# Encoder block on one core: neighbourhood attention in four shifted query groups of two key blocks each, and the later modulation as output columns summed on VectorE

## The chip, the cores and the metric

The kernel runs on one core of one Trainium2 chip. The metric is device microseconds of one execution. TensorE is PE in the profile, VectorE DVE, ScalarE ACT, GpSimd POOL, and SyncE, whose queue issues most transfers, SP.

## The reference, cut to what matters

512 tokens of width 2048 pass through one block: a modulation vector from the conditioning `c`, a normalized and modulated input, one projection for two attentions and two gates, the attentions, an output projection, a SwiGLU, and a last norm.

```
mod = c_act @ w_ada + b_ada                     # c_act = silu(c); 6 parts of 2048
sh1, sc1, g1, sh2, sc2, g2 = split(mod, 6)
h  = rms_norm(x, norm1_w) * (1 + sc1) + sh1
qa, ka, va, qb, kb, vb, ga, gb = split(h @ w_in)
ya = global_gqa(...)                            # 8 heads, all 512 keys
yb = neighbourhood_attention(qb, kb, vb, rpb)   # 8 heads: each query sees 8 rows x 16 columns
merged = sigmoid(ga) * (ya @ w_oa) + sigmoid(gb) * (yb @ w_ob)
x  = x + g1 * (merged @ w_out)
h2 = rms_norm(x, norm2_w) * (1 + sc2) + sh2
x  = x + g2 * ((silu(h2 @ w_ffn_gate) * (h2 @ w_ffn_up)) @ w_ffn_down)
return rms_norm(x, final_w)
```

The tokens form a grid of 8 rows and 64 columns. In the neighbourhood attention a query sees all 8 rows and the 16 columns that begin 8 to its left, moved inwards at the grid's edges, with a learned bias by relative row and column.

## The kernel before, in words

Products are made in 32-bit form with a split: each operand is parted into a high part (a copy on ScalarE, line 133) and a rest (a subtraction on VectorE, line 134), and `mm3` makes three products (lines 141 to 143). Weights arrive as `raw` tiles of 128x1024 (512 KB) over SP's queue, are split into `whl`, and are multiplied. `form1` and `form2` are the loops over a weight matrix; behind each weight tile they call `pump`, which advances a background list `bg` by `pace["steps"]` steps and calls functions due from `soon` (a total is put there to run one pump later). A scheduler then sets the order on each engine and mixes independent work, so that the products of the gates and projections stand between those of the attentions. Tokens are in column order: 8 tokens to a grid column, so a block of 128 tokens is 16 columns.

Stages by time in the profile: the first modulation, the norm and the first projections (0 to 300 us), the global attention `att_a` (300 to 430), the gate products `sg_b` (430 to 560), the neighbourhood attention `att_b` with its own projections (560 to 820), more gates (820 to 920), the output projections of both attentions (`gated`, 920 to 1115), `w_out` (1115 to 1300), and the SwiGLU (to the end).

The neighbourhood attention, head by head (`att_b`, lines 635 to 659): four blocks of 128 queries, which see 2, 3, 3 and 2 blocks of keys (`KR`). For each block: three score products of 256 or 384 columns into a bank `S`, scale and bias on VectorE (line 646), a softmax (lines 557 to 568), a 128x128 transposition for each key block (line 650) into bank `T`, and a split into `pt`. Then, key block by key block, three products of 256 or 384 columns into `Y` (lines 656 to 658). The bias of a head is put together on the chip (`bias_of`): 16 transfers of 8 rows each on SP's queue into `braw` (line 625), and three additions of a mask on GpSimd (line 630).

The later modulation (`sh2`, `sc2`, `g1`, `g2`, each 2048 long) is background work of 128 steps. A step loads 1024 columns' worth of `w_ada` (line 285) and multiplies two pieces of 128x512 by a column of `c_act`, adding them into `acc` (line 300, and line 298 for a first piece). So the sum over partitions is still open, and TensorE closes it: `ada_mod.total` with four products of one column for each of 8 groups (line 319), `ada_gate.total` with one product of 512 columns in plain 32-bit form for each of 8 quarters (line 332). The gates are written to memory (line 335) and read back as rows.

The first modulation (line 401) is done in the other way already: rows of transposed weights, `ada1_w`, are multiplied by `call`, which holds `c_act` along the free axis in all partitions, and summed by the same VectorE instruction.

Of the kernel before, what the change touches and what calls it, by code (L numbers as in the profile page):

```python
# [13 lines left out]
F32 = mybir.dt.float32  # L14
F32R = mybir.dt.float32r
AF = mybir.ActivationFunctionType
# [3 lines left out]
P = 128  # L20
# [16 lines left out]
RPB_R, RPB_C = 2 * ROWS - 1, 2 * WIN - 1  # L37
TB_PAD = 240
TB_LEN = 945
TB_RUN = 720  # L40
# [16 lines left out]

def rope_tables():
# [13 lines left out]
def window_masks():  # L72
    def block(i, b0, b1):
        m = np.full((P, (b1 - b0) * P), NEG, np.float32)
        for p in range(P):
            col = i * WIN + p // ROWS
            cs = min(max(col - HALF, 0), GRID_W - WIN)
            for kc in range((i + b0) * WIN, (i + b1) * WIN):
                if cs <= kc < cs + WIN:
                    o = (kc - (i + b0) * WIN) * ROWS  # L80
                    m[p, o:o + ROWS] = 0.0
        return m

    return np.concatenate([block(1, -1, 2), block(0, 0, 2), block(NT - 1, -1, 1)], axis=1)
# [3 lines left out]
def encoder_block(ctx: ExitStack, tc, xp, xT, c, w_ada, ada1_w, b_ada, norm1_w, w_in, q_norm_w, k_norm_w, tb,  # L88
                  w_oa, w_ob, w_out, norm2_w, w_gate, w_up, w_down, final_w, rope, wmask, out):
# [184 lines left out]
    accp = aside  # L274
    def ada_units(cols, w):

        nj = len(cols)
        nk = 1024 // (nj * w)

        for k0 in range(0, KT, nk):  # L280
            raw = raw_tile()
            r4 = raw.rearrange("p (k c n) -> p k c n", k=nk, c=nj)
            for j, col in enumerate(cols):
                src = w_ada[k0 * P:(k0 + nk) * P, col:col + w]
                nc.sync.dma_start(r4[:, :, j], src.rearrange("(k p) n -> p k n", p=P))
            yield [(k0 + e, raw[:, e * nj * w:(e + 1) * nj * w]) for e in range(nk)]

    def ada_acc(cols, w, bias):


        acc = accp.tile([P, 512], F32, tag="acc", name="acc", bufs=2)[:, :len(cols) * w]
        if bias:
            G.memset(acc, 0.0)
            nc.sync.dma_start(acc[0:1, :], b_ada[:, cols[0]:cols[0] + w])
        for parts in ada_units(cols, w):
            for k, part in parts:
                if k == 0 and not bias:
                    V.tensor_scalar(acc, part, cact[:, k:k + 1], None, op0=ALU.mult)
                else:
                    V.scalar_tensor_tensor(acc, part, cact[:, k:k + 1], acc, op0=ALU.mult, op1=ALU.add)  # L300
            yield None
        yield acc

    def ada_done(y, k0, n, s, b_s, nw, t, b_t):
        sl = slice(k0, k0 + n)
        V.tensor_add(s[:, sl], y[:, :n], b_s[:, sl])
        V.tensor_add(t[:, sl], y[:, n:2 * n], b_t[:, sl])
        V.scalar_tensor_tensor(s[:, sl], s[:, sl], 1.0, nw[:, sl], op0=ALU.add, op1=ALU.mult)

    def ada_mod(sh, sc, k0, n, to):  # L310

        for acc in ada_acc((sc + k0 * P, sh + k0 * P), n * P, False):
            if acc is None:
                yield

        def total():
            y = bank("Y")
            for j in range(2 * n):
                nc.tensor.matmul(y[:, j:j + 1], acc[:, j * P:(j + 1) * P], ones[:, 0:1], start=True, stop=True)
            ada_done(y, k0, n, *to)  # L320

        soon.append((1, total))

    def ada_gate(col, q, dst):

        for acc in ada_acc((col + q * 512,), 512, True):
            if acc is None:
                yield

        def total():  # L330
            y = bank("Y")
            nc.tensor.matmul(y, ones, acc, start=True, stop=True)
# [33 lines left out]
    call = p_x.tile([P, D], F32, name="call")  # L366
# [238 lines left out]
    bg.extend(ada_mod(3 * D, 4 * D, k, 2, (s2, b_sc2, n2, t2, b_sh2)) for k in range(0, KT, 2))  # L605
    g1_d, g2_d = ([dram.tile([1, 512], F32, name=f"g{n}d{q}") for q in range(4)] for n in (1, 2))
    bg.extend(ada_gate(2 * D, q, g1_d) for q in range(4))
    bg.extend(ada_gate(5 * D, q, g2_d) for q in range(4))
# [7 lines left out]
    msk = p_b.tile([P, 7 * P], F32, name="msk")  # L616
    nc.sync.dma_start(msk, wmask)
    KR = [(0, 2), (0, 3), (1, 4), (2, 4)]
    MS = [3 * P, 0, 0, 5 * P]

    def bias_of(h):
        raw = p_b.tile([P, 768], F32, tag="braw", name="braw", bufs=1)[:, :TB_RUN]
        for cc in range(WIN):
            o = (WIN - 1 - cc) * RPB_R
            nc.sync.dma_start(raw[cc * ROWS:(cc + 1) * ROWS, :], tb[h * ROWS:(h + 1) * ROWS, o:o + TB_RUN])
# [9 lines left out]
    def att_b(h, q, k, v, vs):  # L635
        bm = bias_of(h)
        pt = [t.rearrange("p (k q) -> p k q", k=NT) for t in pair(p_b, "pt", NT * T, 1)]
        for i in range(NT):
# [10 lines left out]
            for j in range(k1 - k0):  # L649
                nc.tensor.transpose(tp[:, j * P:(j + 1) * P], e[:, j * P:(j + 1) * P], ident)  # L650
# [628 lines left out]
```

## Time and profile before

| | |
|---|---|
| timed runs | 2579.44, 2584.04, 2613.58 us; median 2584.04 |
| span of the profiled execution, first to last instruction | 2582.4 us |
| time of that execution outside its span | not recorded |
| PE busy | 2539.9 us, 98% of the span, 16573 instructions |
| weight loads of PE | 2294.9 us, 89% |
| DVE busy | 1921.5 us, 74% |
| ACT busy | 1026.9 us, 40% |
| POOL busy | 94.6 us, 4% |
| bytes read and written | 412.03 MB and 44.06 MB |

PE's busy time is the union of records that overlap (each matmul's record is longer than its distance to the next), so the distance from one start to the next tells what a product costs. A plain 32-bit product stands as two records.

### The profile page before, as it was taken

The numbers are of one execution on the slowest core, as the hardware profiler recorded it, in microseconds if no ns is written. First come the engines' busy times: TensorE is split into PE (matmuls) and PEld (weight loads), VectorE is DVE, ScalarE is ACT, GpSimd is POOL, SyncE is SP. The second block draws the span as 40 slices with busy tenths as digits, with TensorE's granted clock in tenths as the row PEclk, the third lists the DMA queues.
The fourth block names the chain that finished last, engine by engine and source line by source line (L and its number), as shares of the span: only waits on it lengthen the run. The fifth ranks groups of instructions, "written<-read, shape, count | busy, mean of one in ns | idle before, by whom it ended". The sixth has DMA issues, their size and how long they took to land.

```text
span 2582.4 us, 40993 instructions
## 1 busy us (share of the span) xinstructions
PE 2539.9 (98%) x16573; PEld 2294.9 (89%) x16573; DVE 1921.5 (74%) x2712; ACT 1026.9 (40%) x1404; POOL 94.6 (4%) x134
## 2 busy tenths in 40 slices
PE   7999999999999999999999999999999999999998
PEld 5888878888887887878999999999999998999997
DVE  8985787766645665665798888888888885687867
ACT  5223544223333322225754444444444454334333
POOL 0100000001010000011000000000000000001000
PEclk8999999999999999999999999999999999999999
DMA  9864245975534866776444434443444456547472
GB/s 352 304 227 146 66 155 164 305 235 167 164 100 149 287 219 205 249 256 213 131 139 131 129 120 129 131 129 101 133 130 130 127 192 209 176 144 248 160 256 98
DMA packets 251950, 458.77 MB, mean 178 GB/s; under 512 B 16113, under 2 KB 102497, under 8 KB 243313
## 3 DMA queue, kind: packets, MB, share of 16 engines
q1 hardware_dynamic: 238208, 381.64, 46.2%
q0 software_dynamic: 12064, 71.31, 7.7%
q10 hardware_dynamic: 1488, 3.20, 0.4%
q8 instruction: 130, 2.13, 0.3%
q14 instruction: 60, 0.48, 0.1%
HBM read 412.03 MB, written 44.06 MB: 177 GB/s over the span
## 4 chain that ended last, share of the span: by engine, by line
PE 78%; DMA 7%; DVE 6%; issue 6%; ACT 1%; POOL 0%; SPq 0%; DVEq 0%; POOLq 0%; ACTq 0%
PE mm L141 16%; PE mm L143 16%; PE mm L142 16%; PE S L141 6%; PE S L143 6%; PE S L142 6%; DMA raw<-in_w_ada 4%; PE Y L141 2%; PE Y L142 2%; PE Y L143 2%; DVE whl L134 1%; DVE acc L300 1%; DMA raw<-in_w_down 1%; PE T L143 1%; PE T L141 1%
## 5 line engine op out<-in xcount | busy, mean ns | idle before, releaser
L133 ACT ACTIVATE whl<-raw 128x1024 fp32r<-128x1024 f32 (+1 forms) x483 | 463.9, 962 | 820.1 <-PE mm L143 266.8
L134 DVE TENSOR_TENSOR whl<-raw,whl 128x1024 fp32r<-128x1024 f32 (+1 forms) x483 | 532.0, 1111 | 227.7 <-ACT whl L133 219.2
L300 DVE SCALAR_TENSOR_TENSOR acc<-raw,cact,acc 128x512 f32<-128x512 f32 x248 | 188.2, 759 | 86.3 <-DMA raw<-in_w_ada 79.3
L134 DVE TENSOR_TENSOR whl<-ta,whl 128x1024 fp32r<-128x1024 f32 x104 | 127.3, 1224 | 71.2 <-ACT whl L133 70.0
L133 ACT ACTIVATE whl<-tb 128x1024 fp32r<-128x1024 f32 x104 | 110.7, 1065 | 157.8 <-PE S L143 131.2
L133 ACT ACTIVATE whl<-ta 128x1024 fp32r<-128x1024 f32 x104 | 110.5, 1062 | 150.5 <-PE mm L143 114.0
L134 DVE TENSOR_TENSOR whl<-tb,whl 128x1024 fp32r<-128x1024 f32 x104 | 127.0, 1221 | 11.3 <-ACT whl L133 8.7
L856 DVE TENSOR_TENSOR ta<-raw 128x512 f32<-128x512 f32 x104 | 71.7, 690 | 37.0 <-DMA raw<-in_w_down 34.8
L141 PE MATMUL mm<-whl,s 128*128 128x256 f32 x320 | 88.8, 279 | 4.6 <-DVE acc L1132 4.6
L141 PE MATMUL mm<-x3h,whl 128*128 128x256 f32 x336 | 92.7, 276 | 0.0
L142 PE MATMUL mm<-x3l,whl 128*128 128x256 f32 x336 | 92.7, 276 | 0.0
L143 PE MATMUL mm<-x3h,whl 128*128 128x256 f32 x336 | 92.7, 276 | 0.0
L141 PE MATMUL mm<-x56h,whl 128*128 128x256 f32 x336 | 92.7, 276 | 0.0
L142 PE MATMUL mm<-x56l,whl 128*128 128x256 f32 x336 | 92.7, 276 | 0.0
L143 PE MATMUL mm<-x56h,whl 128*128 128x256 f32 x336 | 92.7, 276 | 0.0
L141 PE MATMUL S<-x56h,whl 128*128 128x256 f32 x336 | 92.7, 276 | 0.0
L142 PE MATMUL S<-x56l,whl 128*128 128x256 f32 x336 | 92.7, 276 | 0.0
L143 PE MATMUL S<-x56h,whl 128*128 128x256 f32 x336 | 92.7, 276 | 0.0
L857 DVE TENSOR_TENSOR ta<-raw,ta 128x512 f32<-128x512 f32 x104 | 71.6, 688 | 27.2 <-DMA raw<-in_w_down 23.1
L142 PE MATMUL mm<-whl,s 128*128 128x256 f32 x320 | 88.9, 278 | 0.0
L143 PE MATMUL mm<-whl,s 128*128 128x256 f32 x320 | 88.7, 278 | 0.0
L858 DVE TENSOR_TENSOR tb<-raw 128x512 f32<-128x512 f32 x104 | 71.6, 688 | 3.4 <-DMA raw<-in_w_down 1.5
(1504 smaller groups left out, 8510.3 us busy)
## 6 DMA issues: line engine op xcount, KB each, us to landing
raw<-in_w_in SPq DMA_DIRECT2D x133, 512.0 KB
raw<-in_w_gate SPq DMA_DIRECT2D x92, 512.0 KB
raw<-in_w_up SPq DMA_DIRECT2D x88, 512.0 KB
raw<-in_w_down SPq DMA_DIRECT2D x88, 512.0 KB
raw<-in_w_ada SPq DMA_DIRECT2D x128, 256.0 KB
raw<-in_w_ada SPq DMA_DIRECT2D x64, 512.0 KB
raw<-in_ada_w POOLq DMA_DIRECT2D x29, 1024.0 KB, 6.5
raw<-in_w_out SPq DMA_DIRECT2D x48, 512.0 KB
```

The source lines that it names most:

```text
L133: S.activation(hi, src, AF.Copy)
L134: eng.tensor_sub(lo, src, hi)
L141: nc.tensor.matmul(o, lh, rh, start=start, stop=False, **kw)
L142: nc.tensor.matmul(o, lh, rl, start=False, stop=False, **kw)
L143: nc.tensor.matmul(o, ll, rh, start=False, stop=stop, **kw)
L300: V.scalar_tensor_tensor(acc, part, cact[:, k:k + 1], acc, op0=ALU.mult, op1=ALU.add)
L856: V.tensor_sub(t1, b12, b11)
L857: V.tensor_sub(t2_, b22, t1)
L858: V.tensor_sub(t3, b22, b12)
```

## The change

**Neighbourhood attention.** The query groups are shifted by 64 tokens: group 0 holds the last 64 and the first 64 tokens, groups 1, 2 and 3 the 128 tokens that straddle two neighbouring key blocks. Each group then sees two key blocks (group 0: blocks 0 and 3). All products of scores and values have 256 columns. Two groups share one bank, so the softmax of a head runs in two passes over 512 columns (with two exponentials of 256 each), in the order (1, 2), (0, 3). The bias with its mask comes ready from memory, one transfer of 128x512 a head on POOL's queue. The queries get 64 more columns, a copy of the last 64 tokens ahead (two ScalarE copies of 64 columns a head). In the value products, the one for key block 2 writes two separate runs of 128 columns of the bank.

**Later modulation.** All four parts are laid out as rows of output columns (`ada2_w`), multiplied by `call` and summed by one VectorE instruction for each 128x1024. Both kinds of total lose their products; the two gates get one transposition of 128x16 each, a transfer of the bias part, an addition, and four stores. `call` moves from a pool of the first stage to `aside`, and is copied once to `call2`.

```diff
+def later_columns(w):
+    return np.concatenate([ada_columns(w[:, 3 * D:5 * D]), w[:, 2 * D:3 * D].T, w[:, 5 * D:].T])
...
-    def ada_acc(cols, w, bias):
...
-                    V.scalar_tensor_tensor(acc, part, cact[:, k:k + 1], acc, op0=ALU.mult, op1=ALU.add)
...
-                nc.tensor.matmul(y[:, j:j + 1], acc[:, j * P:(j + 1) * P], ones[:, 0:1], start=True, stop=True)
...
+    def ada_columns_sum(b0, n):
+        for j in range(b0, b0 + n):
+            for e in range(2):
+                raw = raw_tile()
+                cs = slice(e * 1024, (e + 1) * 1024)
+                nc.sync.dma_start(raw, ada2_w[j * P:(j + 1) * P, cs])
+                V.scalar_tensor_tensor(raw, raw, 1.0, call[:, cs], op0=ALU.mult, op1=ALU.mult,
+                                       accum_out=mcol[:, 2 * j + e:2 * j + e + 1])
                 yield
...
         def total():
-            y = bank("Y")
-            nc.tensor.matmul(y, ones, acc, start=True, stop=True)
+            yp = bank("Y")
+            nc.tensor.transpose(yp[:KT, :P], y, ident)
             o = io.tile([P, 512], F32, tag="io", name="ada_o")
-            V.tensor_copy(o[0:1, :], y[0:1, :])
-            nc.sync.dma_start(dst[q], o[0:1, :])
+            nc.sync.dma_start(o[:KT, :P], row(b_ada[:, col:col + D]))
+            V.tensor_add(o[:KT, :P], o[:KT, :P], yp[:KT, :P])
+            for q in range(4):
+                nc.sync.dma_start(dst[q].rearrange("o (k p) -> (o k) p", p=P), o[4 * q:4 * q + 4, :P])
...
+    bg.extend((ada_mod(), ada_gate(2 * KT, 2 * D, g1_d), ada_gate(3 * KT, 5 * D, g2_d)))
...
     def att_b(h, q, k, v, vs):
-        bm = bias_of(h)
...
+        bm = p_b.tile([P, 512], F32, tag="bm", name="bm", bufs=2)
+        nc.gpsimd.dma_start(bm, bias[h * P:(h + 1) * P, :])
...
+        for gs, b2, o in (((1, 2), inner, 512), ((0, 3), edge, 0)):
             sc = bank("S")
+            for n, g in enumerate(gs):
+                mm3(by(sc)[:, 2 * n:2 * n + 2], *(rows_of(t, g) for t in q), *(keys_of(t, g) for t in k), True, True)
...
+            V.scalar_tensor_tensor(s2v, sc.rearrange("p (g n) -> p g n", g=2), SCALE, b2, op0=ALU.mult, op1=ALU.add)
+            V.reduce_max(mx, s2v, axis=AX.X)
...
+            for j, at in enumerate((0, 1, 2, 3) if o else (2, 3, 1, 0)):
+                nc.tensor.transpose(tp[:, j * P:(j + 1) * P], e[:, at * P:(at + 1) * P], ident)
+            split(*(t[:, o:o + 512] for t in pt), tp)
         yb = bank("Y")
+        for n, (kk, at, to) in enumerate(((1, slice(5, 7), slice(2, 4)), (0, slice(3, 5), slice(1, 3)),
+                                          (2, slice(0, 8, 7), slice(0, 4, 3)), (3, slice(1, 3), slice(0, 2)))):
+            mm3(by(yb)[:, to], v[kk][0][:, vs], v[kk][1][:, vs], *(by(t)[:, at] for t in pt), n == 0, n == NT - 1,
+                skip_group_check=True)
...
+    def queries(hi, lo, b):
+        split(hi[:, 64:], lo[:, 64:], b)
+        for t in (hi, lo):
+            S.activation(t[:, :64], t[:, T:], AF.Copy)
```

Three places show how the change moves instructions. In the new program the same lines of code stand about 2 lower near `split` and `mm3` (131 for 133, 139 to 141 for 141 to 143), 24 lower in the global attention (540 for 564), and 23 lower in `gated` (690 for 713).

The first place is PE in the output projection of the first attention (`y3h` and its like are the split outputs of its heads). Before, a total of a gate stands between two triples:

```order
L143 MATMUL mm<-y3h,whl 128x512
L332 MATMUL Y<-acc,ones 128x512
L141 MATMUL mm<-y4h,whl 128x512
L142 MATMUL mm<-y4l,whl 128x512
L143 MATMUL mm<-y4h,whl 128x512
```

Now there is one of these for all of `g1`, and it is a transposition (`ysum` holds the 16 sums of each partition):

```order
L140 MATMUL mm<-y7l,whl 128x512
L141 MATMUL mm<-y7h,whl 128x512
L306 MATMUL Y<-ident,ysum 16x128
L139 MATMUL mm<-y8h,whl 128x512
L140 MATMUL mm<-y8l,whl 128x512
```

Eight products of 512 columns became two transpositions, and the 32 products of one column (line 319) have no successor on PE.

The second place is DVE at the first two heads of the neighbourhood attention, from the last split of the keys on. Before (`sb` scores with bias, `mx` the maximum, `sm` and `rs` the sum and its reciprocal, `e` the exponentials):

```order
L646 SCALAR_TENSOR_TENSOR sb<-S,bm 128x256
L646 SCALAR_TENSOR_TENSOR sb<-S,bm 128x384
L560 TENSOR_REDUCE mx<-sb 128x1 x2
L561 TENSOR_SCALAR mx<-mx 128x1
L300 SCALAR_TENSOR_TENSOR acc<-raw,cact,acc 128x512
L561 TENSOR_SCALAR mx<-mx 128x1
L134 TENSOR_TENSOR whl<-raw,whl 128x1024
L300 SCALAR_TENSOR_TENSOR acc<-raw,cact,acc 128x512
L566 RECIPROCAL rs<-sm 128x1
L646 SCALAR_TENSOR_TENSOR sb<-S,bm 128x384
L567 TENSOR_SCALAR e<-e,rs 128x256
```

Now, each row over two groups:

```order
L607 SCALAR_TENSOR_TENSOR sb<-S,bm 128x512 x2
L609 TENSOR_REDUCE mx_4850<-sb 128x2
L609 TENSOR_REDUCE mx_4877<-sb 128x2
L610 TENSOR_SCALAR mx_4850<-mx_4850 128x2
L132 TENSOR_TENSOR whl<-raw,whl 128x1024
L610 TENSOR_SCALAR mx_4877<-mx_4877 128x2
L281 SCALAR_TENSOR_TENSOR raw,mcol<-raw,call 128x1024
L615 RECIPROCAL rs_4852<-sm_4851 128x2
L607 SCALAR_TENSOR_TENSOR sb<-S,bm 128x512
L617 TENSOR_SCALAR e<-e,rs_4852 128x256 x2
```

The bias, the maximum and the division of two groups stand together, with the split of a weight tile and one modulation step between them and the first `e` that can be transposed.

The third place is ACT in the global attention (`pth` the split of the transposed exponentials, `st` the split of the values, `g` a gate that `gated` loads and passes through a sigmoid). Before:

```order
L564 ACTIVATE e,sm<-S,mx 128x512
L133 ACTIVATE whl<-raw 128x1024
L133 ACTIVATE pth<-T 128x4x128
L564 ACTIVATE e,sm<-S,mx 128x512
L133 ACTIVATE whl<-raw 128x1024
L133 ACTIVATE pth<-T 128x4x128
```

Now:

```order
L540 ACTIVATE e,sm<-S,mx 128x512
L131 ACTIVATE whl<-raw 128x1024
L690 ACT_TABLE_LOAD
L690 ACTIVATE g<-g 128x512
L131 ACTIVATE pth<-T 128x4x128
L131 ACTIVATE st<-st 128x256
L540 ACT_TABLE_LOAD
L540 ACTIVATE e,sm<-S,mx 128x512
```

Two gates of the later stage `gated` moved up into the attention, and each sigmoid between exponentials brings two table loads. Two further sigmoids (`go`, the gates of `sg_a`) are parted by an exponential where they stood side by side. ACT has 19 table loads in all, where it had 13.

More of the change, by code (lines that the diff above doesn't have):

```diff
@@ L272, in encoder_block @@
     t2 = const.tile([P, KT], F32, name="t2")
[L274 to L286, printed above, removed]
@@ L288, in ada_acc @@
-    def ada_acc(cols, w, bias):
[L291 to L302, printed above, removed]
@@ L324, in ada_gate @@
[L324 to L332, printed above, removed]
+    mcol = const.tile([P, 8 * KT], F32, name="mcol")
+    def ada_columns_sum(b0, n):
[6 more added lines that the diff above has]
+                                       accum_out=mcol[:, 2 * j + e:2 * j + e + 1])
+                yield
@@ L703, in encoder_block @@
     gate = gpool.tile([P, D], F32, name="gate1")
-    accp = gpool
+    first_call, call = call, gpool.tile([P, D], F32, name="call2")
+    S.activation(call, first_call, AF.Copy)
     mx = [pair(p_m, f"m{j}", 1024, 1) for j in range(KT // 2)]
```

140 lines of the change are left out of this document (57 added, 83 removed).

## Prediction

> **What bounds the kernel now.** I read the page first: busy times, then the chain that ended last by engine and by line.
>
> ```profile
> span 2582.4 us, 40993 instructions
> ...
> PE 2539.9 (98%) x16573; PEld 2294.9 (89%) x16573; DVE 1921.5 (74%) x2712; ACT 1026.9 (40%) x1404; POOL 94.6 (4%) x134
> ...
> PE 78%; DMA 7%; DVE 6%; issue 6%; ACT 1%; POOL 0%; SPq 0%; DVEq 0%; POOLq 0%; ACTq 0%
> PE mm L141 16%; PE mm L143 16%; PE mm L142 16%; PE S L141 6%; PE S L143 6%; PE S L142 6%; DMA raw<-in_w_ada 4%; PE Y L141 2%; PE Y L142 2%; PE Y L143 2%; DVE whl L134 1%; DVE acc L300 1%; DMA raw<-in_w_down 1%; PE T L143 1%; PE T L141 1%
> ```
>
> PE is busy for 98% and holds 78% of the chain. One entry speaks against a pure PE bound: the transfers of `w_ada`, which the change touches, have 4% of it, some 106 us. So I asked next what PE itself waited for (us in total, times, longest).
>
> ```profile
> PE Y L259 <- DMA xnT<-in_xT: 5.8, 1, 5.8
> ...
> PE T L583 <- DVE rs L566: 0.7, 1, 0.7
> ...
> PE mm L143 <- DVE whl L134: 0.2, 1, 0.2
> ```
>
> These are the first, one from the middle and the last of a list of 18 that adds up to 31 us, and no row of it names `w_ada`. The windows over stages (length, then busy time and instructions of PE, its weight loads, DVE, ACT and POOL) say the same of the stage in which the chain runs through these transfers, and show the one place where ACT is full.
>
> ```profile
> 300.00:320.00 20.00, 19.95 (x100) 15.53 (x99) 16.42 (x48) 19.02 (x49) 0.00 (x0) 1.00 0.09 27
> 820.00:1025.00 205.00, 203.38 (x889) 166.15 (x888) 125.51 (x160) 67.15 (x86) 1.06 (x2) 1.00 0.75 241
> ```
>
> From 820 to 1025 us PE starts 889 products in 205 us, one each 0.231 us. In the dense run at the end of the next fence it is 0.23 us. So the chain's walk through transfers there is a tie that PE nearly wins, and work removed from PE counts.
>
> **The totals of the modulation.** Each row is a start, a length and the instruction; "x8" are eight records in a row.
>
> ```profile
> 446.69 0.95 PE L319 MATMUL Y<-ones,acc 128*128 128x1 f32 x8
> 447.50 0.49 PE L141 MATMUL mm<-h12h,whl 128*128 128x512 f32 x1
> 447.82 0.40 PE L142 MATMUL mm<-h12l,whl 128*128 128x512 f32 x1
> ...
> 1035.46 1.02 PE L332 MATMUL Y<-acc,ones 128*128 128x512 f32 x2
> 1035.92 0.79 PE L141 MATMUL mm<-y4h,whl 128*128 128x512 f32 x1
> 1036.55 0.39 PE L142 MATMUL mm<-y4l,whl 128*128 128x512 f32 x1
> 1036.78 0.40 PE L143 MATMUL mm<-y4h,whl 128*128 128x512 f32 x1
> ```
>
> A product of 512 columns takes 0.23 us to the next start (1036.55 to 1036.78). From the start of the eight records of line 319 to the second product behind them pass 1.13 us, less one product 0.90 us. The code has eight such groups: **7.2 us**. A total of a gate takes 1.09 us less 0.23, so 0.86 us, and two gates of four quarters have eight of them: **6.9 us**. All fall away. Two transpositions of 16 rows come instead. The trace has none of that shape; the nearest are the 128x128 ones below (0.11 us) and, as the upper end, a whole total (0.86 us). I take 0.2 us each for the transposition and the break in the stream, **0.4 us** for both.
>
> **The neighbourhood attention.** One head's mix with the stream of products:
>
> ```profile
> 599.17 0.49 PE L650 MATMUL T<-ident,e 128*128 128x128 f32 x3
> 599.41 0.42 PE L141 MATMUL S<-qkh 128*128 128x384 f32 x1
> 599.67 0.34 PE L142 MATMUL S<-qkl,qkh 128*128 128x384 f32 x1
> 599.85 0.33 PE L143 MATMUL S<-qkh,qkl 128*128 128x384 f32 x1
> 600.02 0.40 PE L143 MATMUL mm<-h5h,whl 128*128 128x512 f32 x1
> ...
> 602.47 0.28 PE L141 MATMUL S<-qkh 128*128 128x256 f32 x1
> 602.59 0.28 PE L142 MATMUL S<-qkl,qkh 128*128 128x256 f32 x1
> ```
>
> A product of 384 columns takes 0.175 us (599.67 to 600.02 for two), one of 256 takes 0.12. By the code a head has two wide blocks of queries and two wide blocks of keys, three products each; over eight heads that is 96 products, times 0.055 us **5.3 us**. The number of products stays. Three transpositions and a product of 384 take 0.50 us (599.17 to 599.67), so a transposition takes (0.50 - 0.175) / 3 = 0.11 us; eight a head instead of ten, 16 in all, save **1.8 us**.
>
> Eight heads have one value product triple each that writes two runs of 128 columns. Nothing of this form is in the trace. Below it is bounded by a plain 256 (no cost), above by two products as long as a transposition of 128 columns, 0.22 us instead of 0.12, so 24 times 0.10 or 2.4 us. I take no cost, since runs of 128 elements are nearer to one run than to single elements. The Trainium skill, "PSUM — Partial Sum Buffer", section "Specifications (TRN2)", says that any non-contiguous access pattern in PSUM slows matmuls significantly, which speaks against this edit; no run here shows it yet, and by it the sum would be up to 2.4 us smaller.
>
> **Will VectorE and ScalarE keep up?** In the modulation steps VectorE gets lighter.
>
> ```profile
> L300 DVE SCALAR_TENSOR_TENSOR acc<-raw,cact,acc 128x512 f32<-128x512 f32 x248 | 188.2, 759 | 86.3 <-DMA raw<-in_w_ada 79.3 <-DMA g<-sgb 1.7 <-DMA braw<-in_tb 0.8
> L401 DVE SCALAR_TENSOR_TENSOR raw<-raw,call 128x2048 f32<-128x2048 f32 x32 | 72.8, 2286 | 0.0
> L401 DVE DVE_READ_ACCUMULATOR raw<-raw,call 128x1 f32 x32 | 2.7, 84 | 0.0
> ```
>
> A step was two of 0.759 us, 1.52; it becomes one of half of 2.286 plus 0.084, 1.23 us. Over 128 steps that is 37 us less, hidden under PE: it gains nothing. Bytes stay the same in longer runs, 64 transfers of `w_ada` and 128 of the bias leave SP's queue, and eight come to POOL's: also nothing, since SP and POOL have 0% of the chain. The copy into `call2` (2048 columns, an estimated 2.8 us as four of the 0.69 us exponentials below) and four small copies for each pair of heads fall on ACT, which is busy for 40% of the span, behind the global attention.
>
> Two things get worse. The first is the order on VectorE at a pair of heads, shown above. Before, it went like this:
>
> ```profile
> 588.63 0.51 PE L141 MATMUL S<-qkh 128*128 128x256 f32 x2
> ...
> 595.31 0.38 PE L650 MATMUL T<-ident,e 128*128 128x128 f32 x2
> ...
> L560 DVE TENSOR_REDUCE mx<-S 128x1 f32<-128x512 f32 x32 | 21.8, 685 | 3.0 <-PE S L143 2.9
> ```
>
> From the first score to the first transposition passed 6.7 us, filled with products. Now VectorE does, until the first transposition can start: two biases and two maxima of 512 (taken as the last row, four times 0.69), a weight split and a modulation step of 1024 columns (taken as 1.23 each), a third bias 0.69, two divisions (0.35 each, half a 512 row), and four small ones of some 0.1: 7.0 us, and it begins 0.7 us after the first score (six products of 0.12). I assume that the overlaps of neighbouring records at ten joints make up for that, so 7.0 us. PE's order has 15 score products and 20 of 512 columns in that time, 1.8 + 4.6 = 6.4 us. The gap of 0.6 us occurs at the two pairs of heads where a modulation step stands there; without the step the chain is covered. **1.2 us** lost; bounds 0 and 0.6 for all 16 passes, 9.6.
>
> The second is the table loads in the global attention, where ACT is full (19.02 of 20 us).
>
> ```profile
> 300.88 1.28 ACT L564 ACT_TABLE_LOAD   x1
> 302.18 0.69 ACT L564 ACTIVATE e<-S,mx 128x512 f32<-128x512 f32 x1
> ```
>
> A switch costs ACT 1.3 us (300.88 to 302.18). Behind the load waits an exponential, behind it the division and the transposition. Six more are 7.7 us of ACT. PE's only recorded wait of that kind in the global attention is the 0.7 us of line 583, while the program has three loads near it: 0.23 us a load, so **1.4 us** for six; bounds 0 and 7.7. The Trainium skill, "ScalarE: Activation LUTs", section "What ACT_TABLE_LOAD costs", gives a load of about 1283 ns and a drain of about 1380 ns, 2.66 us for each switch. The row agrees with the load and shows no drain of that size; by the page's sum six switches would take 16 us of ACT and might cost PE that much.
>
> **The sum.** 7.2 + 6.9 + 5.3 + 1.8 = 21.2 us saved, 0.4 + 1.2 + 1.4 = 3.0 us lost: 18.2 us. The span becomes 2564.2 us. What lies around it isn't recorded; the median of the timed runs stands 1.6 us over the span, and I carry that over: **2566 us**, 0.7% less. The half of the run that follows `w_out` keeps its order, so nothing comes or goes there.
>
> **The rivals.**
>
> *The passes over 512 columns hold PE up* (the slower side). Place: `att_b`, 16 passes, VectorE's row of two biases, two maxima and two divisions ahead of each transposition. Without this mechanism 21.2 - 1.8 = 19.4 us are gained, so it decides at 1.2 us of wait a pass. If each pass comes 2 us late (the 1.4 us of two more 512 rows and 0.6 from above), 32 us are lost: 2584 - 19.4 + 32 = 2597 us. Against it: a head's columns through each of VectorE's operations fall from 1280 to 1024, with half as many instructions on single columns, and products of the next projection stand between. 6%.
>
> *The stage from 820 to 1115 is paced by transfers after all*, as the chain says. Then the totals of the gates return nothing: 2566 + 6.9 = 2573 us. For it: 4% of the chain and 79 us of VectorE's waits; against it: PE's 0.231 us a product. 13%.
>
> *Each table load stops PE in full*: 7.7 in place of 1.4 us, 2572 us. For it: ACT at 95%; against it: line 583's 0.7 us. 10%.
>
> *The change doesn't shorten what it says*, because products of 256 columns are held to the pace of weight loads (2294.9 us for 16573 loads, 0.138 us each): 0.037 in place of 0.055 us, 96 times, 1.8 us less, 2568 us. Against it: the distance of 0.12 us above. It lies inside the forecast's own range.
>
> *More is gained*: the losses of 3.0 us stay out, and with VectorE lighter by 37 us and half as many passes a third of PE's 31 us of waits goes too: 2566 - 3 - 10 = 2553 us. 9%.
>
> **How the numbers follow.** The forecast, 18 us gained give or take 6 (2560 to 2572, with the bounds of unknown costs), has 62%; the rivals as given. The range takes in the faster case and the three partial ones and, with 9.6 + 7.7 + 2.4 us of upper bounds in place of 1.2 + 1.4 + 0, ends at 2566 + 17 = 2583; below, it ends at 2553, the faster case. A measurement of this kernel can tell about 2%, 52 us, from no change. No case with a price reaches that on the faster side (2% for what I overlooked); on the slower side only the first rival with waits of 4.5 us a pass would (72 - 19.4 = 53 us; 3%). Same: 95%.
>
> **What would show it.** No records of one column behind the start and no total of 512 columns; no product of 384 columns, and 0.12 us from one of 256 to the next; the steps of VectorE at 1.15 us with a read of 0.08; PE's waits for `T` in the attentions under 3 us in total; 19 table loads. The prediction is wrong if PE's waits in `att_b` exceed 10 us, or if the second half of the run changes its length.

## The result: 17 us slower, with less work on PE

| | before | after |
|---|---|---|
| median of the timed runs | 2583.39 us (21 runs) | 2600.58 us (21 runs, 2595.0 to 2632.34) |
| ratio to before, 95% interval | | 1.0088, 1.0064 to 1.0113 |
| span of the profiled execution | 2582.4 us | 2600.8 us |

The forecast was 2566 us. The difference is under the 2% that the prediction counts as a change, but its interval leaves out 1. In some executions of nearly every kernel PE's products from some 1300 to 2100 us come more slowly at a granted clock of 1.00 (4248 instead of 4414 from 1500 to 2000 us), which adds some 30 us; the medians include them, which lifts those of the kernel before by 0.1 to 3.4 us, and the profiles of e6, e7, e12 and e13 are such ones, so that of these only windows ahead of 1115 us are read.

The page of after, in the parts that were shown of before (span, busy times, chain by engine and by line):

```profile
span 2600.8 us, 40427 instructions
...
PE 2525.2 (97%) x16479; PEld 2278.5 (88%) x16479; DVE 1867.5 (72%) x2608; ACT 1031.7 (40%) x1419; POOL 73.4 (3%) x110
...
PE 71%; DMA 13%; DVE 7%; issue 6%; ACT 2%; SPq 0%; POOL 0%; DVEq 0%; ACTq 0%; POOLq 0%
PE mm L139 14%; PE mm L141 14%; PE mm L140 14%; DMA raw<-in_ada_w 9%; PE S L139 5%; PE S L141 5%; PE S L140 5%; PE Y L139 2%; PE Y L140 2%; PE Y L141 2%; DVE whl L132 2%; DMA raw<-in_w_down 2%; PE T L141 1%; PE T L139 1%; PE T L140 1%
```

Every engine but ACT has less to do, PE by 14.7 us and VectorE by 54, and yet the span grew: the chain now spends 9% instead of 4% in the modulation's transfers and 7% instead of 6% on VectorE. (`in_ada_w` stands here for `ada2_w`.) The windows by stage show where: first before, then after (length; PE, its weight loads, DVE, ACT, POOL; granted clock; DMA share; GB/s).

```profile
480.00:560.00 80.00, 80.00 (x366) 66.57 (x365) 60.04 (x80) 19.11 (x21) 3.14 (x3) 1.00 0.88 286
560.00:620.00 60.00, 60.00 (x296) 49.68 (x295) 39.72 (x85) 22.15 (x40) 2.85 (x4) 1.00 0.60 185
820.00:920.00 100.00, 99.77 (x435) 81.25 (x435) 60.47 (x74) 36.19 (x47) 0.53 (x1) 1.00 0.84 272
920.00:1020.00 100.00, 100.00 (x440) 82.21 (x440) 63.01 (x83) 28.84 (x37) 0.53 (x1) 1.00 0.68 219
1500.00:2000.00 500.00, 500.00 (x4414) 500.00 (x4413) 424.53 (x527) 219.29 (x230) 0.00 (x0) 1.00 0.41 126
```

```profile
480.00:560.00 80.00, 63.45 (x271) 49.95 (x269) 42.17 (x59) 16.12 (x19) 0.00 (x0) 0.96 0.76 250
560.00:620.00 60.00, 56.80 (x259) 46.87 (x260) 35.28 (x55) 17.42 (x32) 0.92 (x2) 0.95 0.59 183
820.00:920.00 100.00, 96.02 (x422) 77.49 (x421) 49.12 (x69) 35.43 (x52) 0.00 (x0) 0.98 0.74 233
920.00:1020.00 100.00, 92.99 (x405) 75.09 (x405) 54.73 (x78) 25.87 (x33) 0.00 (x0) 1.00 0.66 206
1500.00:2000.00 500.00, 500.00 (x4414) 500.00 (x4413) 423.93 (x526) 217.90 (x229) 0.00 (x0) 1.00 0.41 127
```

PE idles 19.8 us between 480 and 620 us, and 11.0 us between 820 and 1020, nearly all of it at products of gates and projections, which the change doesn't touch. Behind the first idle time the granted clock is 0.96 and 0.95. The second half runs at the same pace, 4414 products in 500 us. DMA is *less* busy where PE idles (0.76 instead of 0.88 from 480 to 560 us), so it isn't a larger load on DMA that holds PE up. PE's waits (us in total, times, longest) name VectorE:

```profile
PE mm L139 <- DVE vl L132: 12.5, 1, 12.5
PE mm L141 <- DVE whl L132: 9.7, 7, 2.7
PE mm L140 <- DVE whl L132: 6.6, 7, 1.6
```

All three are subtractions of a split. Why is VectorE late with them when it has less work? The longest wait, instruction by instruction (start, length, engine, line; in brackets its idle time before and what ended it): VectorE, then SP's issues, then PE.

```profile
550.88 1.23 DVE L281 SCALAR_TENSOR_TENSOR raw<-raw,call 128x1024 f32<-128x1024 f32 x1 [4.25 <-DMA raw<-in_ada_w]
552.03 0.08 DVE L281 DVE_READ_ACCUMULATOR raw<-raw,call 128x1 f32 x1
552.03 1.22 DVE L132 TENSOR_TENSOR whl<-raw,whl 128x1024 fp32r<-128x1024 f32 x1
556.26 1.23 DVE L281 SCALAR_TENSOR_TENSOR raw<-raw,call 128x1024 f32<-128x1024 f32 x1 [3.01 <-DMA raw<-in_ada_w]
...
561.31 1.23 DVE L281 SCALAR_TENSOR_TENSOR raw<-raw,call 128x1024 f32<-128x1024 f32 x1 [2.68 <-DMA raw<-in_ada_w]
...
562.46 2.48 DVE L132 TENSOR_TENSOR vl<-mm,vh 128x512 fp32r<-128x512 f32 x4
```

```profile
552.14 0.33 SPq L280 DMA_DIRECT2D raw<-in_ada_w  x1
...
557.52 0.33 SPq L280 DMA_DIRECT2D raw<-in_ada_w  x1
```

```profile
550.33 0.39 PE L141 MATMUL mm<-whl,h15l 128*128 128x512 f32 x1
563.20 0.79 PE L139 MATMUL mm<-h0h,whl 128*128 128x512 f32 x1 [12.48 <-DVE vl L132]
```

The last product of the value projection starts at 550.33 and takes 0.39 us, and ScalarE has the high parts `vh` ready at 551.36; the split `vl` needs nothing more. But in VectorE's queue two modulation sums stand ahead of it whose transfers are not even issued yet: SP issues one at 552.14, when the sum before it has freed a raw buffer, and it is summed at 556.26; the next is issued at 557.52 and summed at 561.31. Each link (free a buffer, issue, land, sum, free) takes some 5 us, and VectorE sits in it, in order, with work behind it that could run. The Trainium skill, "Perfetto Trace Analysis", section "Tensor Engine Instruction (MATMUL, LD_WEIGHTS)", calls VectorE's queue strictly first in, first out; this trace agrees, by the 12.48 us.

The same order costs PE something in the global attention: PE is busy for 106.81 of the 110 us from 320 to 430, where it was for 109.01. A sum waits for its transfer, behind it stands the maximum `mx` of a softmax (at 379.84), and the exponential and PE's next scores wait for that:

```profile
378.69 1.23 DVE L281 SCALAR_TENSOR_TENSOR raw<-raw,call 128x1024 f32<-128x1024 f32 x1 [2.22 <-DMA raw<-in_ada_w]
...
380.02 0.69 ACT L540 ACTIVATE e<-S,mx 128x512 f32<-128x512 f32 x1 [2.08 <-DVE mx L537]
...
380.86 0.50 PE L139 MATMUL S<-kh,qh 128*128 128x512 f32 x1 [0.81 <-ACT e L540]
```

How did this order stand before? Take one weight tile of the gate stage: SP's issue of the tile and of the steps' transfers next to it, then VectorE's queue up to the tile's split. First the kernel before:

```profile
487.47 2.34 SPq L285 DMA_DIRECT2D raw<-in_w_ada  x4
490.49 0.37 SPq L148 DMA_DIRECT2D raw<-in_w_in  x1
...
493.90 2.33 DVE L300 SCALAR_TENSOR_TENSOR acc<-raw,cact,acc 128x512 f32<-128x512 f32 x3
496.67 1.23 DVE L134 TENSOR_TENSOR whl<-raw,whl 128x1024 fp32r<-128x1024 f32 x1 [0.45 <-ACT whl L133]
```

Now after:

```profile
486.67 0.38 SPq L146 DMA_DIRECT2D raw<-in_w_in  x1
490.12 2.91 SPq L280 DMA_DIRECT2D raw<-in_ada_w  x2
...
494.33 1.23 DVE L281 SCALAR_TENSOR_TENSOR raw<-raw,call 128x1024 f32<-128x1024 f32 x1 [0.52 <-DMA raw<-in_ada_w]
...
498.16 1.23 DVE L281 SCALAR_TENSOR_TENSOR raw<-raw,call 128x1024 f32<-128x1024 f32 x1 [2.60 <-DMA raw<-in_ada_w]
...
499.31 1.22 DVE L132 TENSOR_TENSOR whl<-raw,whl 128x1024 fp32r<-128x1024 f32 x1
```

Before, the tile issued at 490.49 is split behind sums whose transfers were issued ahead of it (SP's four of 487.47 are two steps). After, the tile issued at 486.67 is split behind two sums whose transfers are issued *behind* its own, at 490.12 and 492.70. I call such sums early. (The tiles and sums are matched with SP's issues by their order in the trace; a step of before is two instructions of VectorE.) The early sums of two or more steps stood ahead of 3 of 23 weight splits from 430 to 560 us and of 3 of 22 from 560 to 700 us before, and of 20 of 20 and 21 of 22 after. This order is in the program, like the orders shown with the change, and could have been read before the run.

The theories at this point: **A**, the order on VectorE; **B**, the new transfer itself (one of 512 KB instead of two of 256) or too few buffers for it; **C**, the neighbourhood attention. A further one, **D**, came up in the second pair of runs.

### The profile page after: what moved, and what is told of

Same layout as the page of the kernel before. It is cut to its first block, busy times and chain, and to the rows that moved or that the text cites. A ratio compares the mean times of both kernels' runs of the same rounds, so it can differ in the third digit from the quotient of the medians.

```text
span 2600.8 us, 40427 instructions
## 1 busy us (share of the span) xinstructions
PE 2525.2 (97%) x16479; PEld 2278.5 (88%) x16479; DVE 1867.5 (72%) x2608; ACT 1031.7 (40%) x1419; POOL 73.4 (3%) x110
## 4 chain that ended last, share of the span: by engine, by line
PE 71%; DMA 13%; DVE 7%; issue 6%; ACT 2%; SPq 0%; POOL 0%; DVEq 0%; ACTq 0%; POOLq 0%
PE mm L139 14%; PE mm L141 14%; PE mm L140 14%; DMA raw<-in_ada_w 9%; PE S L139 5%; PE S L141 5%; PE S L140 5%; PE Y L139 2%; PE Y L140 2%; PE Y L141 2%; DVE whl L132 2%; DMA raw<-in_w_down 2%; PE T L141 1%; PE T L139 1%; PE T L140 1%
## 5 line engine op out<-in xcount | busy, mean ns | idle before, releaser
L281 DVE SCALAR_TENSOR_TENSOR raw<-raw,call 128x1024 f32<-128x1024 f32 x128 | 157.3, 1229 | 198.3 <-DMA raw<-in_ada_w 197.5
L131 ACT ACTIVATE whl<-tb 128x1024 fp32r<-128x1024 f32 x104 | 110.7, 1065 | 157.1 <-PE S L141 134.0
```

What stands on the lines that cost most here:

```text
L131: S.activation(hi, src, AF.Copy)
L281: V.scalar_tensor_tensor(raw, raw, 1.0, call[:, cs], op0=ALU.mult, op1=ALU.mult, accum_out=mcol[:, 2 * j + e:2 * j + e + 1])
```

## The experiments

Times are medians; the kernel before, timed alongside, had 2583 to 2585 us. Code cuts show the main lines of an edit.

### e1: the sums pinned behind what is written ahead of them

```
-  V.scalar_tensor_tensor(raw, raw, 1.0, call[:, cs], ...)
+  tc.keep_in_program_order(V.scalar_tensor_tensor(raw, raw, 1.0, call[:, cs], ...))
```

> The changed kernel, with each modulation sum of VectorE (line 281 of the changed kernel) pinned behind the instructions written ahead of it for VectorE, so that no sum of a later step stands ahead of the split of an earlier weight tile. Transfers, tiles, buffers and operations stay. Theory A (order): PE was held up because in VectorE's queue two sums of later steps stand ahead of each weight split from 430 to 560 us, and one or two from 820 us on, and wait there for transfers that were issued behind that weight tile; then PE's idle time and low clock between 480 and 620 us and between 820 and 1020 us go (36 us), and the time is 2562 to 2572 us. Theory B (the transfers): a transfer of 512 KB in rows of 4 KB comes later than two of 256 KB, or the ring of four raw buffers is too short for it, whatever the order; then the time stays at 2590 to 2605 us. Theory C (the neighbourhood attention holds PE up): also 2590 to 2605 us.

**2574.11 us**, ratio to before 0.9971 (0.9947 to 0.9995). Nothing but the order changed, and 26 us came back. B and C fall as sole causes. It stays above A's range since the pin also put sums behind the attention's results, and a new wait came up at 805 us:

```profile
PE mm L139 <- ACT whl L131: 5.8, 1, 5.8
```

### e2 and e3: each part alone; e5 and e6: the same, with the addresses put back

e2 and e3 are the kernel before with one part of the diff. e5 and e6 add one unused tile:

```
+  const.tile([P, 32], F32, name="level")     # e5; in e6 96 columns
```

> The kernel before with the neighbourhood attention of the changed kernel alone; the modulation is the old one (two transfers of 256 KB a step, sums into acc, totals on PE). The 128 small bias transfers leave SP's queue. In VectorE's order two sums of later steps now stand ahead of the weight split in the second half of the stage from 430 to 560 us, where before there were none or one. Theory A (order): 7 us gained on PE, less a stall of some 5 to 15 us in that stage: 2577 to 2592 us, with VectorE waiting for w_ada ahead of the splits there. Theory B (the transfers of the new modulation): the old transfers have no such wait, 2573 to 2579 us. Theory C (the neighbourhood attention): 2600 us or more.

> The kernel before with the new modulation alone (transposed columns, one transfer of 512 KB a step, row sums on VectorE, no totals on PE); the neighbourhood attention is the old one, with its 128 small bias transfers on SP. In VectorE's order two later sums stand ahead of some 17 weight splits in the first half of the stage from 430 to 560 us and none to two behind. Theory A (order): 14 us gained on PE, less stalls of 10 to 25 us: 2580 to 2596 us. Theory B (the transfers): 14 us gained, less the full 36 us: 2602 to 2610 us. Theory C (the neighbourhood attention): 2568 to 2572 us.

> The neighbourhood attention alone as in e2, with one unused tile of 128 bytes a partition behind the constants, so that the tiles on the left side of the on-chip memory (hT, the operands of w_out and of the SwiGLU) begin at the same offset modulo 512 bytes as before (256; in e2 128). Theory D (address): in e2 and e3 products of 256 columns of the second half took 115.9 and 117.9 ns instead of 113.3 because those tiles begin at another offset; then the pitch returns to 113.3 ns, the second half loses its 28 us, and the time is 2580 to 2602 us. Without D the time stays at 2625 to 2632 us. Of what is left against before, theory A (order) expects stalls ahead of weight splits from 500 to 560 us, so more than the 2576 us that the sum of the savings gives.

> The new modulation alone as in e3, with an unused tile of 384 bytes a partition behind the constants, so that the left side's tiles begin at the offset of before modulo 512 bytes (256; in e3 384). Theory D (address): pitch back to 113.3 ns from 117.9, the second half shorter by 36 us, 2585 to 2610 us. Without D: 2640 to 2650 us. Theory A (order): stalls of 10 to 25 us before 620 us stay, so the time is above the 2570 us of the sum.

**e2 2629.25 us, e3 2645.91 us** (1.0192 and 1.0241): far slower than both parts together. e2 lies where C has it, e3 in no theory's range. **e5 2584.95 us, e6 2599.88 us** (0.9966 and 1.0015, intervals 0.9928 to 1.0005 and 0.997 to 1.006): the unused tile gave 44 and 46 us back. The window from 1500 to 2000 us of e2, then of e5:

```profile
1500.00:2000.00 500.00, 500.00 (x4281) 500.00 (x4281) 412.25 (x510) 211.93 (x223) 0.00 (x0) 1.00 0.39 120
```

```profile
1500.00:2000.00 500.00, 500.00 (x4414) 500.00 (x4413) 425.10 (x528) 219.00 (x230) 0.00 (x0) 1.00 0.41 125
```

PE never waits in either, but e2 gets through 133 products fewer at the full clock. Each part grows the constants (e2 by 384 bytes a partition, e3 by 640), and so moves the operands on the left side of the on-chip memory; with the unused tile the growth is 512 bytes in e5 and 1024 in e6, and the pace of before is back. (These bytes, and the 256, 128 and 384 modulo 512 of the expectations, are counted from the tiles in the programs; no profile shows an address.) SP, PE, VectorE and ScalarE run the same instructions in the same order in e2 and e5, and in e3 and e6. Both parts together add 1024 bytes and keep the pace: the change was lucky. That is D, tested by itself in e9. With the addresses level, the attention alone is no slower, so C falls, and the modulation alone has the stalls: e6's window from 480 to 560 us has 66.37 us of PE.

### e4: two transfers of 256 KB; e12: five buffers

```
-  nc.sync.dma_start(raw, ada2_w[j * P:(j + 1) * P, cs])
+  for c in (0, 512):
+      nc.sync.dma_start(raw[:, c:c + 512], ada2_w[j * P:(j + 1) * P, e * 1024 + c:e * 1024 + c + 512])
```

```
-  wbufs = {"raw": 4, "w": 3, "at": 0}
+  wbufs = {"raw": 5, "w": 3, "at": 0}
```

> The changed kernel, with each modulation transfer of 128x1024 made as two transfers of 128x512 (256 KB each, rows of 2 KB), as the kernel before had two a step. VectorE's order stays as in the changed kernel. Theory A (order): the stalls stay, 2595 to 2610 us. Theory B (the size of the transfer): the stalls go, 2562 to 2580 us. Theory C: 2590 to 2605 us.

> The changed kernel with five raw buffers instead of four in the first half (room made by one instead of two buffers for the gates' and for the attentions' results on their way to memory; the second half has five as before). The sums stay unpinned, and three to five of later steps now stand ahead of each split. Theory R (the ring is too short for the new transfers): the stalls go, 2562 to 2575 us. Theory A (order): a longer ring lets the sums run further ahead, each still waiting for its own transfer ahead of the split; 2588 to 2615 us.

**e4 2609.03 us, e12 2596.96 us** (1.0126 and 1.0072): both as A expects. Neither the size of the transfer nor the number of buffers is the cause; with five buffers more sums stand early, and PE has 66.68 of the 80 us from 480 to 560.

### e7 and e11: the order of after, forced upon the kernel before

```
   raw, _ = unit(w, k0, nk, c0, ncol)
+  for _ in range(pace.get("ahead", 0)):
+      advance()                         # the steps, ahead of the split
   ...
+  if pace.get("ahead"):
+      tc.keep_in_program_order(rest)    # rest: the subtraction of the split
```

> The kernel before with nothing of the change, only its order on VectorE made like that of the changed kernel in the gate stage and the first value projection: the two modulation steps of a pump are written between the load and the split of its weight tile, and the split is pinned behind them, so two sums stand ahead of some 17 weight splits, each waiting for transfers issued behind that weight tile. Theory A (order): PE stalls from 450 to 560 us, 2592 to 2612 us. Theory B (only the new transfers stall): 2580 to 2588 us.

> The kernel before with the order of e7, but from the gate stage on through to the end of the output projections of the attentions (430 to 1070 us) and not only to 560 us: every modulation step is written between the load and the split of a weight tile, with the split pinned behind it. e7 lost nothing although its splits came 6.3 us apart instead of 5.6 in the gate stage; theory A says that the weight tiles split ahead for PE (three buffers) absorbed it. A: with the order kept up for longer this stock is used up and PE stalls, 2592 to 2615 us. If order alone cannot stall the old kernel, 2578 to 2588 us, and something of the new modulation is needed for it.

**e7 2587.05 us** (1.0002, 0.9965 to 1.004): a miss for A as I had put it. The splits did fall behind, 6.3 us apart instead of 5.6 (14 intervals from 453 to 541 us), but from 541 on, where e7's early sums end, they came at 543, 547, 551 and 554 us. In after they went on at 552, 557, 565 and 572 us. So early sums alone are not enough: they must last until PE's lead, the split tiles in stock, is used up. In e7 a weight tile was split at 491.84 us and PE came to it at 495.09; seven tiles later it was 535.57 and 535.04, so the lead was gone just when the early sums ended. In after it was gone at the first of these tiles already, which was split at 493.81 while PE came at 492.25, sooner because it no longer makes the totals (three groups of 0.9 us from 432 us on). Before 541 us it had waited six times, 6.2 us in all. **e11 2643.67 us** (1.0232) is above both of its ranges. It kept the early sums up to the end (its edit differs from the one shown: the steps of a pump are held back and written at the next weight tile), but its pin also put splits behind the attention's own steps; it waits for `ptl` and `e` too, and tells nothing about A.

### e8: each sum behind its own pump's weight split, and nothing else

```
+  def behind_split(sums):               # order alone: no wait
+      tc.add_manual_dep(sums.ins, last_split[0].ins.name, DependencyInfo(NoSync, DATA))
...
-  V.scalar_tensor_tensor(raw, raw, 1.0, call[:, cs], ...)
+  behind_split(V.scalar_tensor_tensor(raw, raw, 1.0, call[:, cs], ...))
```

> The changed kernel, with each modulation sum queued on VectorE behind the split of the weight tile of its own pump, and behind nothing else (in e1 behind every instruction written ahead of it, such as the splits of the attention's results). Theory A (order): as e1 in the gate stage, without the wait of 5.8 us at 805 us that e1 had where its sums stood behind the first two attention results; 2562 to 2572 us. Should it come out above e1 (2574 us), then what e1 lost at 805 us wasn't due to the pin.

**2561.3 us** (2560.71 to 2564.57), ratio 0.9865 (0.9804 to 0.9925): 39 us faster than the changed kernel, the fastest of all and just below A's range. The edit pins only VectorE's queue, but the scheduler answered with some changes elsewhere (ScalarE has 17 table loads instead of 19). Its windows:

```profile
480.00:560.00 80.00, 75.53 (x324) 61.85 (x324) 48.41 (x68) 17.77 (x20) 0.00 (x0) 0.96 0.82 273
560.00:620.00 60.00, 59.87 (x293) 49.44 (x292) 35.30 (x62) 21.09 (x43) 1.07 (x2) 1.00 0.58 181
820.00:920.00 100.00, 100.00 (x443) 82.81 (x442) 58.35 (x77) 33.57 (x43) 0.00 (x0) 1.00 0.83 266
920.00:1020.00 100.00, 100.00 (x443) 82.72 (x442) 61.25 (x85) 30.29 (x36) 0.00 (x0) 1.00 0.70 225
1500.00:2000.00 500.00, 500.00 (x4414) 500.00 (x4413) 421.73 (x523) 219.07 (x231) 0.00 (x0) 1.00 0.41 125
```

VectorE's wait for the modulation's transfers from 430 to 560 us, of after and of e8 (us, times, longest):

```profile
DVE raw L281 <- DMA raw<-in_ada_w: 60.3, 30, 5.2
```

```profile
DVE raw L287 <- DMA raw<-in_ada_w: 16.4, 16, 2.1
```

From 480 to 620 us one wait of size is left, 4.5 us for `vl` at 540 us.

### e9 and e10: the address by itself, and the pin by itself

e9 is e8 with e6's unused tile of 96 columns; e10 is the kernel before with `behind_split`, as in e8, around its sums (lines 298 and 300).

> The kernel of e8, with an unused tile of 384 bytes a partition behind the constants, so that the left side's tiles begin at 128 modulo 512 bytes, as in e2, instead of 256. Nothing else moves. Theory D (address): the products of 256 columns in the second half rise from 113.3 ns to 115.5 or more in nearly every run, and the time from 2561 to 2580 to 2600 us. If the addresses of e2 and e3 were not the reason, 2559 to 2566 us.

> The kernel before with nothing of the change, each modulation sum queued behind the split of its own pump's weight tile as in e8. Theory A (order): its order in the gate stage was already so, hence little: 2574 to 2586 us. If the pin is a gain of its own that has nothing to do with the change, it is as large as from the changed kernel to e8: 2545 to 2560 us.

**e9 2612.21 us** (1.0099, 1.0071 to 1.0127; all 12 runs from 2601.91 to 2618.74): 51 us more than e8 from 384 bytes that nothing reads, with every instruction of SP, PE, VectorE and ScalarE in the same order. That is D, and more than the range it gave. The window from 1500 to 2000 us has e2's pace, at e2's offset:

```profile
1500.00:2000.00 500.00, 500.00 (x4280) 500.00 (x4279) 413.18 (x511) 211.35 (x222) 0.00 (x0) 1.00 0.40 123
```

The slower pace begins early: from 100 to 250 us PE has 645 products in e2, e3 and e9, and 663 or 664 in every other kernel of this document, busy for all 150 us in each.

**e10 2584.91 us** (0.9997, 0.9962 to 1.0031): the pin gains nothing without the change. It mends what the change's order broke.

### e13 and e14: pinned to 810 us only, from 810 us only

> The changed kernel with the sums queued behind the splits as in e8, but only for the steps up to the end of the neighbourhood attention (to 810 us). From there the order is that of the changed kernel, with one or two sums ahead of a split, much as in the kernel before. Theory A with a stock: the waits of PE from 820 to 1020 us (some 11 us in the changed kernel) follow from the stock of split tiles that the earlier stalls used up; then this equals e8, 2559 to 2567 us. Theory A without it: the late waits have their own order as cause and stay, 2570 to 2580 us.

> The changed kernel with the sums queued behind the splits only for the steps from 810 us on; up to there the order is that of the changed kernel. With a stock that is carried over: the stalls between 480 and 620 us stay and the late ones too, 2595 to 2602 us. With causes of their own: only the early stalls stay (26 us with the lower clock), 2582 to 2590 us.

**e13 2578.04 us** (0.9956, 0.9911 to 1.0001), **e14 2580.94 us** (0.998, 0.9937 to 1.0022). e13 is as A without a stock expects, e14 1 us below its range. With neither 2600.58 and with both 2561.3, the early pin is worth 20 to 23 us and the late one 17 to 20. Windows from 820 to 1020 us of e13, then from 480 to 560 and 820 to 1020 us of e14:

```profile
820.00:920.00 100.00, 95.33 (x410) 77.16 (x409) 51.60 (x69) 27.96 (x36) 0.00 (x0) 0.98 0.76 240
920.00:1020.00 100.00, 95.99 (x419) 77.78 (x418) 57.53 (x81) 29.48 (x37) 0.00 (x0) 1.00 0.66 212
```

```profile
480.00:560.00 80.00, 66.97 (x281) 52.77 (x279) 42.48 (x59) 16.57 (x19) 0.00 (x0) 0.96 0.77 250
...
820.00:920.00 100.00, 100.00 (x456) 82.25 (x456) 58.16 (x83) 38.04 (x58) 0.00 (x0) 1.00 0.80 255
920.00:1020.00 100.00, 100.00 (x443) 82.69 (x442) 61.19 (x84) 30.80 (x37) 0.00 (x0) 1.00 0.70 225
```

Each stage's stalls go with its own pin and stay without it. The idea of a carried-over stock falls.

### e15 and e16: each part with level addresses and the pin

> The neighbourhood attention alone, at the left side's offset of before (e5), with the old modulation's sums queued behind the splits as in e10. Against e10 (2585 us) this is the attention's part of the prediction's sum: 5.3 + 1.8 - 1.2 - 1.4 = 4.5 us, so 2577 to 2584 us. A rival: the attention brings more than the sum says, because its biases leave SP's queue; 2565 to 2574 us.

> The new modulation alone, at the left side's offset of before (e6), with its sums queued behind the splits. Against e10 (2585 us) this is the modulation's part of the sum: 7.2 + 6.9 - 0.4 = 13.7 us, so 2568 to 2574 us. A rival: the totals on PE were worth less (other products hid them), 2578 to 2584 us.

**e15 2573.63 us, e16 2578.15 us** (0.9965, 0.9925 to 1.0006; 0.998, 0.993 to 1.0029). Both miss their ranges and lie in the rivals'. Against e10 that is 11 us for the attention instead of 4.5, and 7 for the modulation instead of 13.7; with such intervals the two can't be told apart, and the sum's split between them isn't confirmed. The profiles help a little. In e15 PE is busy for all 260 us from 560 to 820, in e10 for 257.4. In e16 PE still idles 4.5 us from 480 to 560 us (75.51 busy) and 2.8 from 820 to 920 (97.18), where e10 has 80.00 and 99.67; with them its part would be some 14 us, by estimate. Where the rest of the attention's surplus comes from stays open. The pin matters to the attention alone too: e5, the same without it, took 2584.95 us.

## Why the prediction was wrong, step by step

- **What bounds the kernel: right.** PE does, and its work shrank as counted: 16573 records became 16479.
- **The terms of the sum: right in size together, not shown one by one.** With the order mended, e8 stands 24 us under the kernel before (2561.3 against 2585.22, timed alongside; some 21 with 3.4 us taken off that median), e10's pin being worth nothing; the forecast was 18. That the attention came out above its part and the modulation below it (e15, e16) cancels in this. The totals are gone. The two transpositions of 16 rows lengthen the stream by 0.11 us each (three products and one of them take 0.80 us, the three alone 0.69), where the prediction took 0.2. Value products that write two runs of 128 columns start 0.12 us apart, like the plain ones. Of a head's twelve these are the seventh to the ninth (the first three rows), with a plain one behind them:

```profile
629.21 0.28 PE L139 MATMUL Y<-pth,vh 128*128 128x256 f32 x1
629.33 0.28 PE L140 MATMUL Y<-ptl,vh 128*128 128x256 f32 x1
629.45 0.28 PE L141 MATMUL Y<-pth,vl 128*128 128x256 f32 x1
629.57 0.28 PE L139 MATMUL Y<-pth,vh 128*128 128x256 f32 x1
```

  So the Trainium skill's rule on non-contiguous access in PSUM ("PSUM — Partial Sum Buffer", "Specifications (TRN2)") is not seen for runs of 128 elements, and taking no cost was right.
- **The passes over 512 columns and the table loads: costs of 2.6 us that weren't there as such.** PE is busy for 200.00 of the 200 us from 620 to 820 in after. There are 19 table loads as counted, of 1283 ns each. PE does lose 3.2 us from 320 to 430 us, but most of its waits there lead to sums that wait for their transfers, as shown above. With these pinned (e8, with 17 table loads) PE is busy for 109.78 of the 110 us.
- **"In the modulation steps VectorE gets lighter ... it gains nothing": the step that failed.** The sums did get lighter, 1.23 us and 0.08 for the read, with 54 us less on VectorE in all. I weighed how long they take and not where they stand. The place that I examined in VectorE's order was the pair of heads; the stage with two steps a pump, where the change had moved sums ahead of splits, I took as hidden from its busy time. In place of no effect, the runs showed a loss: with two early sums ahead of nearly every split PE idles, and putting each sum behind its split is worth 39 us (after against e8). With it fell "also nothing, since SP and POOL have 0% of the chain", on the moved transfers, at least as a rule: e5 has the old modulation and no bias transfers on SP, and early sums of two or more steps ahead of 18 of 21 splits from 560 to 700 us, where the kernel before has 3 of 22; the pin gained it 11 us (e15). Whether the moved transfers or another part of the attention's edit turned that order over wasn't tried.
- **"The chain's walk through transfers there is a tie that PE nearly wins": true of before, and the warning.** The tie was lost: PE idles 11.0 of the 200 us from 820 to 1020. In the gate stage the change made VectorE fall behind by 0.9 us a tile (20 splits from 430 to 560 us instead of 23).
- **The rivals: none had it.** The slower one named PE's wait for VectorE but put it in `att_b`, at the wrong queue position; that its 2597 us is near the measured 2600.58 is luck. The rival of paced transfers had the place from 820 us on, but priced a lost gain and not a stall. The two tests of the prediction (waits in `att_b` over 10 us; the second half changing) both passed while the time was wrong: they guarded the places I had thought of, and the first passes only because most of the wait of 12.5 us falls ahead of 560 us.
- **Open.** From 810 to 1065 us the early sums of two or more steps stand ahead of 18 of 45 splits before and of 19 of 42 after, and only after stalls there to speak of; e14 shows that the order is needed for it, not what else. That the schedule flipped by the two parts is seen; why the scheduler flipped it wasn't tried.

## What to carry to other kernels

A lighter instruction that waits for a transfer can cost more than a heavy one, if it stands in an in-order queue ahead of work that is ready. When a change touches what a scheduler orders, compare the queue of every engine in the stages where transfers are close to PE's pace, and ask of each waiting instruction whether its transfer is issued before or behind what stands after it. When a part alone is slower than the whole, look at the addresses before the logic.

## What the hardware showed that I had not expected

The pace of TensorE's products in a stage without any wait depends on where their operands lie: 4414 products in 500 us with the left side's tiles where they were or moved by 512 or 1024 bytes, 4281 with them moved by 384 (e2) and 4280 by 1408 (e9), at a granted clock of 1.00 in each. An unused tile of 384 bytes a partition cost 51 us in all (e8 against e9), more than the change could have gained. e3 (moved by 640) had 4248. Only these shifts were run, so no rule for other addresses follows.
